# Turned SwiGLU values finished behind later weight tiles, and embedding products kept in DRAM

## The chip, the cores and the metric

The kernel runs on one core of a Trainium2 chip. The metric is device time in microseconds (us) of one execution, as a median of several runs. The engines are named as in the profile: PE multiplies matrices (PEld is its loading of stationary operands), DVE and ACT are the vector and the scalar engine, POOL is the general one, and SP issues most of the DMAs.

## The reference

A trunk of two layers is computed for one sequence of 256 tokens with 1024 channels, in float32. Layer 0 has a mixer (a gated convolution and a gated delta rule), a dense SwiGLU and a gated per-layer embedding; layer 1 has a mixer (differential attention and a convolution module), a SwiGLU with eight experts of which each token uses two, and again a gated embedding. The change lies in the experts and in the embedding of layer 1:

```python
def swiglu(hn, w_gate_up, w_down):
    g, u = jnp.split(hn @ w_gate_up, 2, axis=-1)
    return (jax.nn.silu(g) * u) @ w_down

# each expert e of 8: w_gate_up[e] is 1024 x 7168, w_down[e] is 3584 x 1024
y = lax.map(expert_block, (rows, blk_e))          # swiglu of the rows of expert e
out = jnp.zeros((T, D)).at[tok_s].add(y[dest] * g_s[:, None])

def per_layer_embed(h, p_i, g_norm, w_proj, w_gate):
    gate = jax.nn.sigmoid(rmsnorm(h, g_norm) @ w_gate)
    return (p_i @ w_proj) * gate
```

## The kernel before

All weights come from DRAM once, in tiles of 1 MB (`raw`, 11 buffers), on SP's DMA queue. Products are made with float32 numbers split in two parts of a shorter format: `wsplit` (L135 ff.) lets ACT copy 1024 columns into the high part (`wh`, names h_...) and DVE subtract it to get the low part (`wl`, names l_...). Each of the two has four buffers, which come free when PE has used them. A tile of weights thus costs one ACT copy, one DVE subtraction and several PE products.

The experts run one after the other, each in four chunks of hidden channels (`CHUNKS`: 1024, 1024, 1024, 512). Experts 0 to 3 hold up to 128 tokens ("many"): three products for each tile (high with high, high with low, low with high). Experts 4 to 7 (`FEW`) hold up to 64 tokens, and both parts of the tokens stand beside each other as 128 columns, so that two products do.

A step (e, c) of the loop (L1340 ff.) has two halves. `gate_up` multiplies the tokens with the gate and up weights of chunk c, channel tile by channel tile (k = 0 to 7), into PSUM tiles mg and mu. Then `down` multiplies the values of the chunk before with its down weights (names d..., tiles y). In between stands `mid`, called at k = `MID` = 1, which works on the values of the chunk before (`h_T`):

- many: PE transposes the values (tile mt, L1220), ACT and DVE split them (mhh, mhl, L197 and L198);
- few: ACT has copied gate and up out of PSUM (msg, msu, L1188); PE turns both with small matmuls against `both`, which also adds the two parts (tile mt), four pieces for each of gate and up; ACT takes Silu (mgu, L1211), DVE multiplies (mgu, L1212), and both split the product (mh, L197 and L198). A block is 512 channels, so a chunk of 1024 has two blocks, mt520 and mt521 for expert 5, chunk 2.

The scheduler sets the order on each engine from the order in which the program issues the work and from priorities; an engine runs its instructions strictly in that order, so one that waits holds all behind it. `after(...)` pins an instruction behind a named one. The turn of the chunk (e, c) thus lies in the step after it, among the down tiles of the chunk before (e, c): mt520 is made in step (5, 3) while the tiles d5_1 are being multiplied, and h_T's instructions stand on ACT and DVE in the midst of the copies and splits of these tiles.

The embedding products p @ w_proj of layer 1 (pj1, four tiles of 128 x 512) are made near the start of the experts, are copied to SBUF by ACT (L387) and stay there in four of the twelve `s2` buffers until the end. The last down block (r_dl, L1264) and the gate weights of the embedding (r_pg, r_pg1h) follow behind the experts.

Of the kernel before, what the change touches and what calls it, by code (L numbers as in the profile page):

```python
# [24 lines left out]
NE = 8  # L25
# [58 lines left out]
def trunk_kernel(  # L84
# [6 lines left out]
    pe, act, dve, pool, sync = nc.tensor, nc.scalar, nc.vector, nc.gpsimd, nc.sync  # L91
# [5 lines left out]
    dr = ctx.enter_context(tc.tile_pool(name="dr", bufs=1, space=bass.MemoryType.DRAM))  # L97
# [75 lines left out]
    def mm(o, a, b, start, stop, shared=False):  # L173
        last["mm"] = pe.matmul(o, a, b, start=start, stop=stop, skip_group_check=shared)  # L174
# [768 lines left out]
    def layer1_moe(pT):  # L943
# [110 lines left out]
        def few(e):  # L1054
            return e >= FEW
# [106 lines left out]
        def products(e, triples, start, stop):  # L1162


            if not few(e):
                return mm3s(triples, start, stop)
            for part in range(2):
                for o, a, b in triples:
                    mm(o, a, b[part], start and part == 0, stop and part == 1)

        def gate_up(e, c, mid):
            ns = CHUNKS[c][1] // 512
            banks = [[pa(f"m{nm}{e}{c}{i}") for i in range(ns)] for nm in "gu"]
            for k, j, wt in gate_up_weights(e, c):
                if (k, j) == (MID, 0):
                    mid()
                products(e, [(banks[j][i], tokens[e][k], sub2(wt, slice(None), slice(i * 512, i * 512 + 512))) for i in range(ns)],
                         k == 0, k == KT - 1)

            def activate():  # L1180

                res = []
                with after("wcopy", "wsplit"):
                    for i in range(ns):
                        if few(e):
                            res.append([s2(f"ms{nm}{e}{c}{i}", [P, 512]) for nm in "gu"])
                            for j in range(2):
                                act.copy(res[i][j], banks[j][i])  # L1188
                            continue
                        sg = s2(f"msg{e}{c}{i}", [P, 512])  # L1190
                        act.activation(sg, banks[0][i], AF.Silu)
                        dve.tensor_tensor(sg, banks[1][i], sg, MUL)
                        res.append(sg)
                return res

            return activate

        def h_T(e, c, sgs):

            res = []  # L1200

            for i, sg in enumerate(sgs):
                if few(e):

                    q = pt(f"mt{e}{c}{i}", (P, 2, 4, P // 2))
                    for j in range(2):
                        for g in range(2):
                            for k in range(2):
                                mm(q[:, j, 2 * g + k, :], sg[j][:, 256 * g + k : 256 * g + 256 : 2], both, True, True)
                    t = s2(f"mgu{e}{c}{i}", [P, 4, P // 2])  # L1210
                    act.activation(t, q[:, 0], AF.Silu)  # L1211
                    dve.tensor_tensor(t, q[:, 1], t, MUL)  # L1212
                    hT = s2(f"mh{e}{c}{i}", [P, 4, 2, P // 2], F32R)
                    split((hT[:, :, 0], hT[:, :, 1]), t)
                    res += [hT[:, k].rearrange("q i s -> q (i s)") for k in range(4)]
                    continue
                q = pt(f"mt{e}{c}{i}", (P, 4, P))
                for g in range(2):
                    for k in range(2):
                        pe.transpose(q[:, 2 * g + k, :], sg[:, 256 * g + k : 256 * g + 256 : 2], ident)  # L1220
                hT = (s2(f"mhh{e}{c}{i}", [P, 4, P], F32R), s2(f"mhl{e}{c}{i}", [P, 4, P], F32R))
                split(hT, q)
                res += [sub2(hT, slice(None), k) for k in range(4)]
            return res

        def down(e, c, hT, yb, between):

            c0, n = CHUNKS[c]
            res = None
            for g in range(n // 256):  # L1230
# [3 lines left out]
                for i in range(2):  # L1234
                    products(e, [(yb[half], hT[2 * g + i], sub2(wt[i], slice(None), HALF[half])) for half in range(2)],
                             c == g == i == 0, c == len(CHUNKS) - 1 and g == n // 256 - 1 and i == 1)
                if g == n // 512 - 1 and between:
                    res = between()
            return res
# [100 lines left out]
        prev = None  # L1340
        for e in range(NE):
            for c in range(len(CHUNKS)):
                if e % 2 == 1 and c == 2 and e <= FEW - 1:
                    spread_slots = gather(e // 2 + 1)
                if (e, c) == (FEW, 1):
                    spread_slots()

                def mid():
                    if prev:
                        hT[prev] = h_T(*prev, sg)  # L1350
                    if (e, c) == (0, LATE):
                        for bn in todo:
                            product(*bn, pt)
                            copy(*bn)

                activate = gate_up(e, c, mid)
                if prev:
                    sg = back(*prev, activate)
                else:
                    sg = activate()  # L1360
                    with after("wsplit"):
                        gates()
                prev = e, c
# [129 lines left out]
```

## Time and profile before

| | |
|---|---|
| median of 3 runs | 1497.5 us (1496.99 to 1498.06) |
| profiled execution | 1497.28 us, of which span 1495.5 us |
| PE busy | 1444.5 us (97%) |
| PEld busy | 1194.7 us (80%) |
| DVE busy | 1268.0 us (85%) |
| ACT busy | 1076.1 us (72%) |
| DMA | 438 MB, mean 293 GB/s |
| granted PE clock | 0.995 |

The span is the profiled part of one execution; the rest, 1.8 us, lies around it. A busy share is a mean over stretches with different limits, so the rows further down are taken by stretch: the experts 0 to 3 lie at about 530 to 1005 us, the experts 4 to 7 at about 1005 to 1450 us. In a timeline, a row "x6" is six instructions of one kind in a row; the time in brackets is how long the engine was idle before, and behind the arrow stands what released it.

### The profile page before, as it was taken

The numbers are of one execution on the slowest core, as the hardware profiler recorded it, in microseconds if no ns is written. First come the engines' busy times: TensorE is split into PE (matmuls) and PEld (weight loads), VectorE is DVE, ScalarE is ACT, GpSimd is POOL, SyncE is SP. The second block draws the span as 40 slices with busy tenths as digits, with TensorE's granted clock in tenths as the row PEclk, the third lists the DMA queues.
The fourth block names the chain that finished last, engine by engine and source line by source line (L and its number), as shares of the span: only waits on it lengthen the run. The fifth ranks groups of instructions, "written<-read, shape, count | busy, mean of one in ns | idle before, by whom it ended". The sixth has DMA issues, their size and how long they took to land.

```text
span 1495.5 us, 22012 instructions
## 1 busy us (share of the span) xinstructions
PE 1444.5 (97%) x7726; PEld 1194.7 (80%) x7726; DVE 1268.0 (85%) x1716; ACT 1076.1 (72%) x1441; POOL 4.9 (0%) x14
## 2 busy tenths in 40 slices
PE   7999999999999999999999999999999999999996
PEld 6999899988888878888888888886766666666665
DVE  6778655556698699999999989989999999999997
ACT  6545544446547678887887877779988988988975
POOL 0000000000000000000000000000000000000000
PEclk9999999999999999999999999999999999999998
DMA  9614656555452469898898998999999999999961
GB/s 350 241 43 131 216 177 196 172 195 185 147 203 106 149 248 354 327 410 333 322 376 336 392 347 341 359 363 389 377 409 414 390 413 410 388 413 408 394 254 44
DMA packets 136610, 438.26 MB, mean 293 GB/s; under 512 B 9067, under 2 KB 34188, under 8 KB 122412
## 3 DMA queue, kind: packets, MB, share of 16 engines
q1 hardware_dynamic: 132960, 433.19, 77.3%
q10 hardware_dynamic: 3148, 2.31, 0.5%
q0 software_dynamic: 384, 1.29, 0.4%
q8 instruction: 62, 1.02, 0.3%
q14 instruction: 56, 0.46, 0.1%
HBM read 434.92 MB, written 1.84 MB: 292 GB/s over the span
## 4 chain that ended last, share of the span: by engine, by line
PE 71%; DVE 18%; issue 4%; ACT 4%; DMA 3%; ACTq 0%; DVEq 0%; POOL 0%; POOLq 0%
PE y L174 14%; PE mg L174 11%; PE mu L174 11%; DVE l L146 11%; PE fu L174 4%; PE fg L174 4%; PE fd L174 4%; PE wo L174 3%; PE pg L174 3%; PE mt L174 2%; DMA r_gu<-in_moe_w_gate_up_dram 2%; DVE l_d L146 2%; PE p L174 1%; PE mt L1220 1%; PE in_og L174 1%
## 5 line engine op out<-in xcount | busy, mean ns | idle before, releaser
L146 DVE TENSOR_TENSOR l<-r_gu,h 128x1024 fp32r<-128x1024 f32 x448 | 526.3, 1218 | 18.1 <-ACT h L145 6.3
L145 ACT CAST h<-r_gu 128x1024 fp32r<-128x1024 f32 x448 | 456.6, 1052 | 60.2 <-PE mu L174 22.4
L146 DVE TENSOR_TENSOR l_d<-r_d,h_d 128x1024 fp32r<-128x1024 f32 x220 | 258.6, 1219 | 16.7 <-ACT h_d L145 10.4
L145 ACT CAST h_d<-r_d 128x1024 fp32r<-128x1024 f32 x220 | 226.8, 1054 | 24.7 <-PE mu L174 10.3
L146 DVE TENSOR_TENSOR l_gu<-r_gu,h_gu 128x1024 fp32r<-128x1024 f32 x44 | 53.8, 1224 | 47.7 <-ACT h_gu L145 47.7
L145 ACT CAST h_gu<-r_gu 128x1024 fp32r<-128x1024 f32 x44 | 46.0, 1048 | 64.2 <-PE fu L174 49.0
L174 PE MATMUL y<-l_d,mh 128*128 128x512 f32 x216 | 75.3, 430 | 3.7 <-DVE l_d L146 3.7
L174 PE MATMUL y<-l_d,mhh 128*128 128x512 f32 x224 | 69.8, 393 | 0.1
L174 PE MATMUL y<-h_d,mh 128*128 128x512 f32 x216 | 69.2, 402 | 0.3
L174 PE MATMUL y<-h_d,mhh 128*128 128x512 f32 x224 | 69.4, 391 | 0.0
L174 PE MATMUL y<-h_d,mhl 128*128 128x512 f32 x224 | 69.1, 390 | 0.0
L174 PEld LDWEIGHTS y<-l_d,mh 128*128 128x128 f32 x216 | 34.4, 188 | 27.4 <-DVE l_d L146 25.1
L146 DVE TENSOR_TENSOR l_fd<-r_fd,h_fd 128x1024 fp32r<-128x1024 f32 x22 | 26.9, 1224 | 27.3 <-ACT h_fd L145 26.3
L174 PE MATMUL fg<-x_ffn0h,h_gu 128*128 128x256 f32 x176 | 49.9, 283 | 0.0
L174 PE MATMUL fu<-x_ffn0h,h_gu 128*128 128x256 f32 x176 | 49.9, 283 | 0.0
L174 PE MATMUL fg<-x_ffn0h,l_gu 128*128 128x256 f32 x176 | 49.9, 283 | 0.0
L174 PE MATMUL fu<-x_ffn0l,h_gu 128*128 128x256 f32 x176 | 49.8, 283 | 0.0
L174 PE MATMUL fu<-x_ffn0h,l_gu 128*128 128x256 f32 x176 | 49.8, 283 | 0.0
L174 PE MATMUL fg<-x_ffn0l,h_gu 128*128 128x256 f32 x176 | 49.8, 283 | 0.0
L174 PEld LDWEIGHTS y<-h_d,mhl 128*128 128x128 f32 x224 | 42.1, 188 | 8.9
L174 PEld LDWEIGHTS y<-l_d,mhh 128*128 128x128 f32 x224 | 41.5, 188 | 9.5 <-DVE l_d L146 1.4
L174 PEld LDWEIGHTS y<-h_d,mhh 128*128 128x128 f32 x224 | 41.8, 188 | 8.9 <-ACT h_d L145 0.4
(719 smaller groups left out, 3673.6 us busy)
## 6 DMA issues: line engine op xcount, KB each, us to landing
r_gu<-in_moe_w_gate_up_dram SPq DMA_DIRECT2D x192, 1024.0 KB, 7.7
r_d<-in_moe_w_down_dram SPq DMA_DIRECT2D x110, 1024.0 KB, 7.7
r_gu<-in_moe_w_gate_up_dram SPq DMA_DIRECT2D x64, 512.0 KB, 6.4
r_gu<-in_ffn_w_gate_up_dram SPq DMA_DIRECT2D x44, 512.0 KB, 4.4
r_fd<-in_ffn_w_down_dram SPq DMA_DIRECT2D x11, 1024.0 KB, 4.9
r_wo<-in_ev_w_out_dram SPq DMA_DIRECT2D x4, 1024.0 KB, 12.8
r_pg<-in_ple_w_gate_dram SPq DMA_DIRECT2D x4, 1024.0 KB, 7.0
r_wo<-in_od_w_out_dram SPq DMA_DIRECT2D x4, 1024.0 KB, 5.0
```

Of the source, the lines that this page charges most:

```text
L145: last["wcopy"] = act.copy(wh, raw[:, i : i + step])
L146: last["wsplit"] = dve.tensor_tensor(wl, raw[:, i : i + step], wh.bitcast(F32), SUB)
L174: last["mm"] = pe.matmul(o, a, b, start=start, stop=stop, skip_group_check=shared)
L1220: pe.transpose(q[:, 2 * g + k, :], sg[:, 256 * g + k : 256 * g + 256 : 2], ident)
```

## The change

`mid` is taken apart into four steps, which a step of the loop calls at four channel tiles of gate and up (`MIDS = (1, 3, 2, 5)`): at k = 1 PE turns the values of a few-token chunk, at k = 3 ACT and DVE make Silu and product, at k = 2 PE transposes the blocks of many-token chunks, and at k = 5 ACT and DVE split. Silu, product and splits are pinned behind the weight copies and splits that were issued last (`after("wcopy", "wsplit")`); the two blocks of a chunk share one tile mgu. A list of blocks (`downs`) takes the place of the loop over chunks; with the numbers given (`RAMP = 0`, `QUAD`, `SLOTS`, `PAIR`) the blocks and the token gathering come in the same order as before. At the end the last chunk is turned outside of the loop. The products pj1 are written to DRAM by ACT's queue at (0, 1), and read again by SP's queue ahead of the last block.

```diff
-        def gate_up(e, c, mid):
+        def gate_up(e, c, at):
...
-                if (k, j) == (MID, 0):
-                    mid()
+                if j == 0 and k in at:
+                    at[k]()
...
-                    t = s2(f"mgu{e}{c}{i}", [P, 4, P // 2])
-                    act.activation(t, q[:, 0], AF.Silu)
-                    dve.tensor_tensor(t, q[:, 1], t, MUL)
-                    hT = s2(f"mh{e}{c}{i}", [P, 4, 2, P // 2], F32R)
-                    split((hT[:, :, 0], hT[:, :, 1]), t)
...
+        def turned(e, c, banks):
+            t = s2(f"mgu{e}{c}", [P, len(banks), 4, P // 2])
+            for i, q in enumerate(banks):
+                act.activation(t[:, i], q[:, 0], AF.Silu)
+                dve.tensor_tensor(t[:, i], q[:, 1], t[:, i], MUL)
+            hidden[e, c] = t
...
+        def h_T(e, c, i, q):
+            if few(e):
+                hT = s2(f"mh{e}{c}{i}", [P, 4, 2, P // 2], F32R)
+                split((hT[:, :, 0], hT[:, :, 1]), hidden[e, c][:, i])
+                return [hT[:, k].rearrange("q i s -> q (i s)") for k in range(4)]
+            hT = (s2(f"mhh{e}{c}{i}", [P, 4, P], F32R), s2(f"mhl{e}{c}{i}", [P, 4, P], F32R))
+            split(hT, q)
+            return [sub2(hT, slice(None), k) for k in range(4)]
...
+            def turn_fresh():
+                if fresh and few(fresh[0]):
+                    banks["fresh"] = turn(*fresh)
+                if now == (0, LATE):
+                    for bn in todo:
+                        product(*bn, pt)
+                        copy(*bn)
+                    for b, i in BLOCKS:
+                        act.dma_start(stored[:, b, i], pj1[b][i])
+            def fresh_turned():
+                if "fresh" in banks:
+                    with after("wcopy", "wsplit"):
+                        turned(*fresh, banks["fresh"])
+            def blocks_across():
+                for d in blocks:
+                    banks[d] = across(*d)
+            def blocks_split():
+                with after("wcopy", "wsplit"):
+                    for d in blocks:
+                        hT[d] = h_T(*d, banks[d])
...
+                activate = gate_up(*now, dict(zip(MIDS, (turn_fresh, fresh_turned, blocks_across, blocks_split))))
...
+        if fresh:
+            turned(*fresh, turn(*fresh))
         last_norm = halves_norm_T("ple1")
-        back(*prev)
+        for b, i in BLOCKS:
+            pj1[b][i] = s2(f"pj1{b}{i}", [P, 512])
+            sync.dma_start(pj1[b][i], stored[:, b, i])
+        hT[downs[0]] = h_T(*downs[0], across(*downs[0]))
+        back(*downs[0])
...
-MID = 1
+MIDS = (1, 3, 2, 5)
+RAMP = 0
+QUAD, SLOTS, PAIR = 14, 17, 6
```

What this does to the order on an engine is shown at three places. On DVE in step (5, 3), the turn of chunk (5, 2), before (l_d5_1_2 and l_d5_1_3 are the splits of the down tiles, l_5_3 those of the gate and up tiles; mgu is the product with Silu, mh the split of it):

```order
L146 TENSOR_TENSOR l_d5_1_2_1_11578<-r_d5_1_2_11571,h_d5_1_2_1_11577 128x1024
L1212 TENSOR_TENSOR mgu520_11633<-mt520_11624,mgu520_11633 128x256
L146 TENSOR_TENSOR l_d5_1_3_0_11592<-r_d5_1_3_11589,h_d5_1_3_0_11591 128x1024
L146 TENSOR_TENSOR l_d5_1_3_1_11596<-r_d5_1_3_11589,h_d5_1_3_1_11595 128x1024
L146 TENSOR_TENSOR l_5_3_0_0_11613<-r_gu5_3_0_11609,h_5_3_0_0_11612 128x1024
L146 TENSOR_TENSOR l_5_3_0_1_11617<-r_gu5_3_0_11609,h_5_3_0_1_11616 128x1024
L198 TENSOR_TENSOR mh520_11636<-mgu520_11633,mh520_11636 128x4x64
L1212 TENSOR_TENSOR mgu521_11648<-mt521_11639,mgu521_11648 128x256
L146 TENSOR_TENSOR l_5_3_2_0_11662<-r_gu5_3_2_11658,h_5_3_2_0_11661 128x1024
L146 TENSOR_TENSOR l_5_3_2_1_11666<-r_gu5_3_2_11658,h_5_3_2_1_11665 128x1024
L198 TENSOR_TENSOR mh521_11651<-mgu521_11648,mh521_11651 128x4x64
```

After:

```order
L146 TENSOR_TENSOR l_d5_1_3_0_11592<-r_d5_1_3_11589,h_d5_1_3_0_11591 128x1024
L146 TENSOR_TENSOR l_d5_1_3_1_11596<-r_d5_1_3_11589,h_d5_1_3_1_11595 128x1024
L146 TENSOR_TENSOR l_5_3_0_0_11613<-r_gu5_3_0_11609,h_5_3_0_0_11612 128x1024
L146 TENSOR_TENSOR l_5_3_0_1_11617<-r_gu5_3_0_11609,h_5_3_0_1_11616 128x1024
L146 TENSOR_TENSOR l_5_3_2_0_11650<-r_gu5_3_2_11646,h_5_3_2_0_11649 128x1024
L146 TENSOR_TENSOR l_5_3_2_1_11654<-r_gu5_3_2_11646,h_5_3_2_1_11653 128x1024
L1216 TENSOR_TENSOR mgu52_11661<-mt520_11624,mgu52_11661 128x256
L1216 TENSOR_TENSOR mgu52_11661<-mt521_11633,mgu52_11661 128x256
L146 TENSOR_TENSOR l_5_3_4_0_11674<-r_gu5_3_4_11670,h_5_3_4_0_11673 128x1024
L146 TENSOR_TENSOR l_5_3_4_1_11678<-r_gu5_3_4_11670,h_5_3_4_1_11677 128x1024
L198 TENSOR_TENSOR mh520_11685<-mgu52_11661,mh520_11685 128x4x64
L198 TENSOR_TENSOR mh521_11688<-mgu52_11661,mh521_11688 128x4x64
```

Both products and both small splits have moved, from the midst of the last down tiles, behind the fourth and the sixth gate and up tile. On ACT the Silus and small copies move in the same way.

On DVE at the turn of chunk (5, 3), in step (6, 0), before:

```order
L146 TENSOR_TENSOR l_d5_2_2_1_11762<-r_d5_2_2_11755,h_d5_2_2_1_11761 128x1024
L1212 TENSOR_TENSOR mgu530_11842<-mt530_11833,mgu530_11842 128x256
L146 TENSOR_TENSOR l_d5_2_3_0_11776<-r_d5_2_3_11773,h_d5_2_3_0_11775 128x1024
L146 TENSOR_TENSOR l_d5_2_3_1_11780<-r_d5_2_3_11773,h_d5_2_3_1_11779 128x1024
L198 TENSOR_TENSOR mh530_11845<-mgu530_11842,mh530_11845 128x4x64
L146 TENSOR_TENSOR l_6_0_0_0_11808<-r_gu6_0_0_11795,h_6_0_0_0_11807 128x1024
L146 TENSOR_TENSOR l_6_0_0_1_11812<-r_gu6_0_0_11795,h_6_0_0_1_11811 128x1024
```

After, with the rows up to the product:

```order
L146 TENSOR_TENSOR l_d5_2_2_1_11761<-r_d5_2_2_11754,h_d5_2_2_1_11760 128x1024
L146 TENSOR_TENSOR l_d5_2_3_0_11775<-r_d5_2_3_11772,h_d5_2_3_0_11774 128x1024
L146 TENSOR_TENSOR l_d5_2_3_1_11779<-r_d5_2_3_11772,h_d5_2_3_1_11778 128x1024
L146 TENSOR_TENSOR l_6_0_0_0_11807<-r_gu6_0_0_11794,h_6_0_0_0_11806 128x1024
L146 TENSOR_TENSOR l_6_0_0_1_11811<-r_gu6_0_0_11794,h_6_0_0_1_11810 128x1024
L146 TENSOR_TENSOR l_6_0_1_0_11825<-r_gu6_0_1_11822,h_6_0_1_0_11824 128x1024
L146 TENSOR_TENSOR l_6_0_1_1_11829<-r_gu6_0_1_11822,h_6_0_1_1_11828 128x1024
L146 TENSOR_TENSOR l_6_0_2_0_11852<-r_gu6_0_2_11849,h_6_0_2_0_11851 128x1024
L146 TENSOR_TENSOR l_6_0_2_1_11856<-r_gu6_0_2_11849,h_6_0_2_1_11855 128x1024
L146 TENSOR_TENSOR l_6_0_3_0_11870<-r_gu6_0_3_11867,h_6_0_3_0_11869 128x1024
L146 TENSOR_TENSOR l_6_0_3_1_11874<-r_gu6_0_3_11867,h_6_0_3_1_11873 128x1024
L1216 TENSOR_TENSOR mgu53_11877<-mt530_11832,mgu53_11877 128x256
```

The product has moved behind eight gate and up tiles of expert 6, and the small split (not in the rows) four tiles further.

On PE at the start of the experts, before (mg and mu are the first gate and up products, oq a transpose):

```order
L174 MATMUL mg000_5574<-h_0_0_1_0_5590,xe0l_5496 128x512
L174 MATMUL mg000_5574<-l_0_0_1_0_5591,xe0h_5495 128x512
L174 MATMUL mg001_5575<-h_0_0_0_0_5400,xe0h_5495 128x512
L174 MATMUL mg001_5575<-h_0_0_0_0_5400,xe0l_5496 128x512
L174 MATMUL mg001_5575<-l_0_0_0_0_5401,xe0h_5495 128x512
L174 MATMUL mg001_5575<-h_0_0_1_0_5590,xe0h_5495 128x512
L174 MATMUL mu000_5576<-h_0_0_0_1_5404,xe0h_5495 128x512
```

After:

```order
L174 MATMUL mg000_5575<-h_0_0_1_0_5591,xe0l_5496 128x512
L174 MATMUL mg000_5575<-l_0_0_1_0_5592,xe0h_5495 128x512
L174 MATMUL pj1_11_5807<-pwh101_5317,pTh1_5152 128x512
L174 MATMUL pj1_11_5807<-pwl101_5318,pTh1_5152 128x512
L174 MATMUL pj1_11_5807<-pwh101_5317,pTl1_5153 128x512
L174 MATMUL pj1_11_5807<-pwh111_5325,pTh1_5152 128x512
L174 MATMUL mg001_5576<-h_0_0_0_0_5400,xe0h_5495 128x512
L174 MATMUL mg001_5576<-h_0_0_0_0_5400,xe0l_5496 128x512
```

Four of the six embedding matmuls of pj1_11 now stand ahead of the products mg001; before, all six stood further on.

## Rows read from the trace of the kernel before

**Rows 1.** Stretches: us; busy of PE, PEld, DVE, ACT, POOL; clock, DMA share, GB/s.

```profile
600.00:1005.00 405.00, 404.85 (x1854) 335.75 (x1853) 376.68 (x371) 320.34 (x349) 0.00 (x0) 1.00 0.93 354
1010.00:1440.00 430.00, 411.08 (x1812) 293.40 (x1811) 412.70 (x411) 378.32 (x457) 0.00 (x0) 1.00 1.01 401
1395.00:1400.00 5.00, 5.00 (x31) 4.42 (x31) 4.07 (x6) 5.00 (x9) 0.00 (x0) 1.00 1.03 430
```

**Rows 2.** Waits, 1005 to 1450: engine, releaser: total us, times, longest.

```profile
ACT mgu L1211 <- PE mt L174: 36.0, 19, 3.4
...
DVE mgu L1212 <- ACT mgu L1211: 8.7, 12, 1.0
...
ACT h L145 <- DMA r_gu<-in_moe_w_gate_up_dram: 0.9, 2, 0.6
```

**Rows 3.** Timeline of DVE in step (5, 3): start, us, operation, [idle before].

```profile
1199.56 6.89 DVE L146 TENSOR_TENSOR l_d<-r_d,h_d 128x1024 fp32r<-128x1024 f32 x6
1207.03 0.42 DVE L1212 TENSOR_TENSOR mgu<-mt,mgu 128x256 f32<-128x256 f32 x1 [0.58 <-ACT mgu L1211]
1207.97 2.36 DVE L146 TENSOR_TENSOR l_d<-r_d,h_d 128x1024 fp32r<-128x1024 f32 x2 [0.51 <-ACT h_d L145]
1210.25 2.37 DVE L146 TENSOR_TENSOR l<-r_gu,h 128x1024 fp32r<-128x1024 f32 x2
...
1215.81 2.35 DVE L146 TENSOR_TENSOR l<-r_gu,h 128x1024 fp32r<-128x1024 f32 x2
```

**Rows 4.** Timeline of PE there: the turn of chunk (5, 2), down products.

```profile
1204.14 0.57 PE L174 MATMUL mt<-both,msg 128*128 128x64 f32 x4
...
1208.73 0.71 PE L174 MATMUL y<-l_d,mh 128*128 128x512 f32 x2
1209.28 0.62 PE L174 MATMUL y<-h_d,mh 128*128 128x512 f32 x2
1209.74 0.63 PE L174 MATMUL y<-l_d,mh 128*128 128x512 f32 x2
```

**Rows 5.** Timeline of ACT there: the first Silu.

```profile
1206.62 0.38 ACT L1211 ACTIVATE mgu<-mt 128x256 f32<-128x256 f32 x1 [2.00 <-PE mt L174]
```

**Rows 6.** Timeline of DVE where chunk (6, 3) is turned.

```profile
1329.45 6.89 DVE L146 TENSOR_TENSOR l_d<-r_d,h_d 128x1024 fp32r<-128x1024 f32 x6
1337.38 0.43 DVE L1212 TENSOR_TENSOR mgu<-mt,mgu 128x256 f32<-128x256 f32 x1 [1.04 <-ACT mgu L1211]
1338.32 2.36 DVE L146 TENSOR_TENSOR l_d<-r_d,h_d 128x1024 fp32r<-128x1024 f32 x2 [0.52 <-ACT h_d L145]
1340.60 0.42 DVE L198 TENSOR_TENSOR mh<-mgu,mh 128x256 fp32r<-128x256 f32 x1
1340.94 5.76 DVE L146 TENSOR_TENSOR l<-r_gu,h 128x1024 fp32r<-128x1024 f32 x5
```

**Rows 7.** Timeline of PE there: the product behind the turn.

```profile
1336.74 0.71 PE L174 MATMUL y<-l_d,mh 128*128 128x512 f32 x2
```

**Rows 8.** Timeline of DVE around the change from expert 3 to 4.

```profile
1005.07 2.35 DVE L146 TENSOR_TENSOR l_d<-r_d,h_d 128x1024 fp32r<-128x1024 f32 x2
1009.84 0.69 DVE L198 TENSOR_TENSOR mhl<-mt,mhh 128x512 fp32r<-128x512 f32 x1 [2.42 <-ACT mhh L197]
...
1013.06 5.76 DVE L146 TENSOR_TENSOR l<-r_gu,h 128x1024 fp32r<-128x1024 f32 x5
```

**Rows 9.** Timeline of PE there: the last down tile of expert 3.

```profile
1013.09 0.63 PE L174 MATMUL y<-h_d,mhl 128*128 128x512 f32 x2
```

**Rows 10.** Timeline of PE at the start of the experts.

```profile
531.11 0.50 PE L174 MATMUL mg<-h,xe0h 128*128 128x512 f32 x1 [0.75 <-ACT pj L387]
```

**Rows 11.** Timeline of SP: DMA issues for the last down block.

```profile
1422.45 3.56 SPq L1264 DMA_DIRECT2D r_dl<-in_moe_w_down_dram  x4
```

**Rows 12.** Timeline of ACT: the first copies of that block.

```profile
1448.56 3.89 ACT L145 CAST h_dl<-r_dl 128x1024 fp32r<-128x1024 f32 x4
```

**Rows 13.** DMA issues on the page: KB each, median us to landing.

```profile
r_d<-in_moe_w_down_dram SPq DMA_DIRECT2D x110, 1024.0 KB, 7.7
```

More of the change, by code (lines that the diff above doesn't have):

```diff
@@ L1196, in gate_up, with turn @@
             return activate
-        def h_T(e, c, sgs):
+        def turn(e, c):
             res = []
[L1202 to L1209, printed above, removed]
-                    t = s2(f"mgu{e}{c}{i}", [P, 4, P // 2])
-                    act.activation(t, q[:, 0], AF.Silu)
-                    dve.tensor_tensor(t, q[:, 1], t, MUL)
-                    hT = s2(f"mh{e}{c}{i}", [P, 4, 2, P // 2], F32R)
-                    split((hT[:, :, 0], hT[:, :, 1]), t)
[L1215 to L1223, printed above, removed]
-            return res
@@ L1226, in down @@
-        def down(e, c, hT, yb, between):
+            for i, sg in enumerate(hidden[e, c]):
+                q = pt(f"mt{e}{c}{i}", (P, 2, 4, P // 2))
+                for j in range(2):
+                    for g in range(2):
+                        for k in range(2):
+                            mm(q[:, j, 2 * g + k, :], sg[j][:, 256 * g + k : 256 * g + 256 : 2], both, True, True)
+                res.append(q)
+            return res
+        def turned(e, c, banks):
[4 more added lines that the diff above has]
+            hidden[e, c] = t
@@ new lines, in across @@
+        def across(e, c, i):
+            if few(e):
+                return None
+            q = pt(f"mt{e}{c}{i}", (P, 4, P))
+            for g in range(2):
+                for k in range(2):
+                    pe.transpose(q[:, 2 * g + k, :], hidden[e, c][i][:, 256 * g + k : 256 * g + 256 : 2], ident)
+            return q
+        def h_T(e, c, i, q):
+            if few(e):
+                hT = s2(f"mh{e}{c}{i}", [P, 4, 2, P // 2], F32R)
[4 more added lines that the diff above has]
+            return [sub2(hT, slice(None), k) for k in range(4)]
@@ L1228, in down @@
+        def down(e, c, i, hT, yb, between):
             c0, n = CHUNKS[c]
-            res = None
-            for g in range(n // 256):
+            for g in range(2 * i, 2 * i + 2):
                 nm = f"d{e}_{c}_{g}"
@@ L1233, in down @@
                 wt = wload(view, (2, D), nm, spare(nm))
[L1234 to L1239, printed above, removed]
+                for k in range(2):
+                    products(e, [(yb[half], hT[2 * (g % 2) + k], sub2(wt[k], slice(None), HALF[half])) for half in range(2)],
+                             c == g == k == 0, c == len(CHUNKS) - 1 and g == n // 256 - 1 and k == 1)
+                if g == 2 * i and between:
+                    between()
         def combine(e, yb, half):
@@ L1249, in combine, with back @@
                 dve.scalar_tensor_tensor(h[:, b, s], q, Gr[:, b, e : e + 1], h[:, b, s], MUL, ADD)
-        yb, hT = {}, {}
+        yb, hT, hidden = {}, {}, {}
         both = sm("both", (P, P // 2))
         dve.tensor_tensor(both, ident[:, : P // 2], ident[:, P // 2 :], ADD)
-        def back(e, c, between=None):
-            if c == 0:
+        def back(e, c, i, between=None):
+            if c == i == 0:
                 yb[e] = [py(f"y{e}{half}") for half in range(2)]
+            part = hT.pop((e, c, i))
             if (e, c) == (NE - 1, len(CHUNKS) - 1):
-                part = hT.pop((e, c))
                 rows = expert(moe_w_down, e)[CHUNKS[c][0] :].rearrange("(g q k) c -> g q k c", k=2, q=P)
@@ L1270, in back @@
                 return
-            res = down(e, c, hT.pop((e, c)), yb[e], between)
+            down(e, c, i, part, yb[e], between)
             if c == len(CHUNKS) - 1:
@@ L1274, in back @@
                     combine(e, yb[e], half)
-            return res
         def more_slots(e, pos):
@@ L1338, in overflow @@
             return over > P, more
[L1340 to L1363, printed above, removed]
@@ L1364, in layer1_moe, with between @@
-        mid()
-        last_norm = halves_norm_T("ple1")
-        back(*prev)
+        gates_up = [(e, c) for e in ORDER for c in range(len(CHUNKS))]
+        downs = [(e, c, n) for e in ORDER for c in range(len(CHUNKS)) for n in range(CHUNKS[c][1] // 512)]
+        stored = dr.tile([P, NB, 2, 512], F32, name="pj1d")
+        fresh = None
+        while gates_up or len(downs) > 1:
+            now = gates_up.pop(0) if gates_up else None
+            step = NE * len(CHUNKS) - len(gates_up) - 1 if now else None
+            n = next((i for i, d in enumerate(downs) if d[:2] not in hidden), len(downs))
+            n = min(1 if now and step < RAMP else 2, n, sum(d[0] == downs[0][0] for d in downs))
+            blocks, downs = downs[:n], downs[n:]
+            if step == QUAD:
+                spread_slots = gather(2)
+            if step == SLOTS:
+                spread_slots()
+            if step == PAIR:
+                gather(1)
+            banks = {}
+            def turn_fresh():
[18 more added lines that the diff above has]
+                        hT[d] = h_T(*d, banks[d])
+            if now:
+                activate = gate_up(*now, dict(zip(MIDS, (turn_fresh, fresh_turned, blocks_across, blocks_split))))
+                def between(now=now, activate=activate):
+                    hidden[now] = activate()
+            else:
+                for f in (turn_fresh, fresh_turned, blocks_across, blocks_split):
+                    f()
+                between = None
+            for i, d in enumerate(blocks):
+                back(*d, between if len(blocks) == 1 else None)
+                if i == 0 and len(blocks) == 2 and between:
+                    between()
+            if not blocks:
+                between()
+            if step == 0:
+                with after("wsplit"):
+                    gates()
+            fresh = now
@@ L1451 @@
 CONV_DVE = (31, 31, 5, 9)
-MID = 1
+MIDS = (1, 3, 2, 5)
+RAMP = 0
+ORDER = (0, 1, 2, 3, 4, 5, 6, 7)
 FEW = 4
+QUAD, SLOTS, PAIR = 14, 17, 6
 X_DVE = (3, 7)
```

## Prediction

> **What bounds the kernel now.** I first cut the run into stretches and read the busy time of each engine in each [rows 1]. In the experts with 128 tokens (600 to 1005 us) the matrix engine PE is busy 404.85 of 405 us: there, no wait of another engine is worth anything. In the experts with 64 tokens (1010 to 1440 us) no engine is full: DVE 412.70, PE 411.08, ACT 378.32 of 430. So what counts there is who waits for whom. The waits [rows 2] show one chain: ACT's Silu (tile mgu, L1211) waits 36.0 us for PE's turn (tile mt), DVE's product waits behind that Silu 12 times for 8.7 us, and each time a weight split l_d waits after it, because ACT could not copy the next h_d while it stood at the Silu. A copy of weights waits for DMA only 0.9 us, so loads do not bound, although the DMA engines are always occupied.
>
> The timelines show one such place in full. In step (5, 3), DVE does six splits from 1199.56, then has 0.58 us of idle time, the product at 1207.03, and 0.51 of idle time [rows 3]; ACT had waited 2.00 us [rows 5]. There are eight of these pairs (the turns of chunks c = 1 and c = 2 of experts 4 to 7). The turn of a c = 3 chunk costs more: 1.04 + 0.52 [rows 6], four times. Turns of c = 0 show no idle time on DVE. Between experts 3 and 4 stands one more of 2.42 us [rows 8].
>
> **The change part by part.**
>
> *The unit.* A split of 1024 columns comes every 1.14 us (two in 1338.32 to 1340.60), a small product or split every 0.34 us (1340.60 to 1340.94) [rows 6]. With these I compare the time a stretch took with its work alone.
>
> *Turns of c = 3.* From 1329.45 to 1340.94 DVE did eight splits, a product and a small split: 8 x 1.14 + 2 x 0.34 = 9.80 of 11.49 us, so 1.69 lost [rows 6]. After the change the small work stands behind eight gate and up tiles of the next expert, and the splits run on. Is there something else that holds them? They need one of four buffers (wl, wh), which PE gives back when it has used the tile. Without the stop, the ninth split would come at 1329.45 + 8 x 1.14 = 1338.57; the fifth tile's product with l_d, which frees its buffer, started at 1336.74 and ended by 1337.45 [rows 7]. So nothing holds them: 1.69 is gained. The last of the four, (7, 3), keeps its old order (there is no next chunk). **3 x 1.69 = 5.1 us.**
>
> *Turns of c = 1 and 2.* From 1199.56 to 1215.81 DVE did 12 splits and 4 small pieces: 12 x 1.14 + 4 x 0.34 = 15.04 of 16.25 us, so 1.21 lost [rows 3]. But this turn has 32 small matmuls, not 16, and PE is at it from 1204.14 to 1208.73, with some products in between [rows 4]. Without the stop DVE ends its eighth split at 1199.56 + 9.12 = 1208.68; the ninth needs the buffer of the fifth tile, whose product y<-l_d starts only at 1208.73 and ends at 1209.44. The tenth needs ACT's copy into the buffer of the sixth tile, free at 1209.90 (y<-h_d from 1209.28); at 1.05 us for a copy alone ([rows 12]: four in 3.89, so 0.95 in a row) it is there by 1210.95. So the ninth ends at 1210.58, the tenth at 1212.09, the twelfth at 1214.37, and with 4 x 0.34 the same work is done at 1215.73 instead of 1215.81. The idle time changes its releaser and stays: 0.1 each, **8 x 0.1 = 0.8 us**. The bounds are 0 and the whole 1.21, eight times 9.7; I take the low end since the products' times are read from this very stretch, where PE did not wait for DVE.
>
> What a rule says to this: repeated idle time on DVE is charged by the trace to ACT's Silu [rows 2]. The Trainium skill, "Perfetto Trace Analysis", § Optimization Strategy, says that the same gap coming again on the engine that should be full can mean too few buffers for the next tile. For c = 1 and 2 this is what the times of PE's products give; for c = 3 they speak against it. By the rule for all places no turn would gain, which is the second rival.
>
> *Between experts 3 and 4.* DVE lost 2.42 before mhl and 0.25 behind it. Afterwards mhl stands behind twelve tiles of expert 4. Here too the buffers set the end: the eighth split from 1005.07 on began at 1013.06 + 3 x 1.14 = 1016.48 [rows 8] without the two stops before it; afterwards it needs the buffer of the last h_d, free when the product that starts at 1013.09 ends, 1013.72 [rows 9], and a copy of 0.95, so 1014.7. 1.8 less the 0.69 of mhl, which comes later, is 1.1; that last product itself waited a little for l_d, which is gone, so I take **1.4 us** (bounds 0 and 2.42 + 0.25 - 0.69 = 2.0).
>
> *Start of the experts.* PE was idle 0.75 us for ACT's copy of pj [rows 10]. In the new order four embedding matmuls of the same length that came later stand there. PE has no other slack until 1005, so **0.75, say 0.8 us** (bounds 0 and 1.1).
>
> *The 128-token experts.* Splits of turned blocks move behind later tiles. PE has 0.15 us of idle time in 405 [rows 1], the count of instructions stays, and the first use is three tiles further on: 0.
>
> *Embedding products in DRAM.* Four writes of 256 KB on ACT's DMA queue near 540 us, and four reads on SP's, which stand among the four loads r_dl and ahead of the last weights r_pg. No row shows a write by ACT; by SP's issues (four in 3.56 us [rows 11]) they take at most 3.6 us of ACT, in a stretch in which ACT is idle a fifth of the time [rows 1] and runs ahead of PE by up to four tiles: 0, bounds 0 and 2. The reads wait for the turn of (7, 2), since they take the buffers of its inputs. That turn is over about two experts of 107.5 us (430 for four) after 1208.73, near 1424. So the loads behind them start some 5 us late, near 1428, and land 8 to 9 later [rows 13]; the first copies of r_dl run at 1448.56 [rows 12]. 11 us are left over: 0.
>
> **Sum:** 5.1 + 0.8 + 1.4 + 0.8 = 8.1. Against the profiled execution's 1497.3 (span 1495.5 and 1.8 around it; median of the runs 1497.5, 0.2 more) that is 1489.2; on the median **1489.4**. By the bounds of all terms: low with 9.7 + 5.1 + 2.0 + 1.1, high with 5.1 less 2.
>
> **The rivals.**
>
> *All the idle time goes.* If the order of PE's products in the turns gives buffers back earlier than I read, 8 x 1.2 + 5.1 + 2.0 + 0.8 = 17.5 are gained: 1480.0. For it: the releaser named in the rows. Against it: the product at 1208.73. DMA would stand it: 401 GB/s become 418 over the stretch, and the fastest of 86 windows of 5 us moved 430 [rows 1].
>
> *The idle time comes back everywhere at the buffers.* Then the turns of c = 3 give nothing either, and only the start and the place between the experts are left: 1497.5 - 2.2 = 1495.3. For it: PE falls behind in every turn. Against it: the release by 1337.45 [rows 7], 1.1 us before it is needed.
>
> *Slower: Silu and split now stand in front of ACT's copies just where DVE takes them from its hand.* At the tenth split of step (5, 3) ACT has no lead at all (above); from there it gains 1.14 - 0.95 = 0.19 a tile, so some 0.8 us at the fourteenth, where two Silus stand together. If that lead were gone, each Silu and small split of 27 blocks would stop DVE for its 0.38 us [rows 5]: 27 x 2 x 0.38 = 20.5, and 1497.5 - 8.1 + 20.5 = 1510. It decides against the change once two fifths of them do so. Against it: ACT has 52 us of idle time in the 430 [rows 1], much of it the waits for the turn that go away.
>
> **How the numbers follow.** My forecast 0.58 (alone 1486 to 1493), all idle time gone 0.18, back at the buffers 0.16, slower 0.08. What a measurement of this kernel can tell from no change is about 0.2%, 3 us. Faster by more: 0.58 + 0.18 = 0.76; within: 0.16; slower by more: 0.08. The range reaches from the first rival to a little above the second, 1480 to 1496, and leaves out the slower case.
>
> **What would show it.** In the trace afterwards: the product behind the Silu no longer in DVE's waits, except at (7, 3); DVE without idle time at the c = 3 turns of experts 4 to 6; at c = 1 and 2 about 0.8 and 0.4 us in front of the first two gate and up splits, released by PE's y products and ACT's copy; PE without the stop for pj. Wrong would be: idle time on DVE behind ACT's Silu or copies at the third to fifth gate and up tile (slower rival), idle time at the c = 3 turns (second rival), or none at c = 1 and 2 (first).

## The result, and the profile after

The changed kernel takes **1488.5 us** (median of 4 runs, 1488.33 to 1488.63) against 1497.5 us before: a ratio of 0.9943, with a 95% interval of 0.9929 to 0.9957. The forecast was 1489.4 us. The profiled execution has a span of 1486.7 us, 8.8 us less than before.

To see where the time went, I took one mark for each expert from the timelines of DVE, the first addition of the expert's result into h (the first row h<-cb of each expert), and set the two traces beside each other. For expert 4 these are the rows, before and after:

```profile
1150.35 1.40 DVE L1249 SCALAR_TENSOR_TENSOR h<-cb,Gr,h 128x512 f32<-128x512 f32 x2
1145.69 1.40 DVE L1260 SCALAR_TENSOR_TENSOR h<-cb,Gr,h 128x512 f32<-128x512 f32 x2
```

| first h<-cb of expert | before, us | after, us | ahead by | gained since the mark above |
|---|---|---|---|---|
| 0 | 675.61 | 674.84 | 0.77 | 0.77 |
| 1 | 800.04 | 799.18 | 0.86 | 0.09 |
| 2 | 920.13 | 918.87 | 1.26 | 0.40 |
| 3 | 1040.73 | 1037.62 | 3.11 | 1.85 |
| 4 | 1150.35 | 1145.69 | 4.66 | 1.55 |
| 5 | 1259.49 | 1253.00 | 6.49 | 1.83 |
| 6 | 1368.60 | 1360.31 | 8.29 | 1.80 |
| 7 | 1456.20 | 1447.82 | 8.38 | 0.09 |
| end of span | 1495.5 | 1486.7 | 8.8 | 0.4 |

Each of the intervals that end at experts 4, 5 and 6 holds one turn of c = 3 and two of c = 1 and 2; the interval of expert 7 holds two turns of c = 1 and 2 and the last turn, which keeps its order. It gains 0.09 us.

The waits between 1000 and 1445 us answer [rows 2] (engine and tile, releaser: total, times, longest). ACT's wait at the Silu for PE's turn has shrunk from 36.0 us to 14.5, and DVE's wait behind that Silu from 12 times to 2. In their place ACT's weight copies wait for PE's y products, and DVE's splits wait for these copies:

```profile
ACT h L145 <- PE y L174: 24.5, 26, 1.3
...
ACT mgu L1215 <- PE mt L174: 14.5, 8, 3.3
...
DVE l L146 <- ACT h L145: 9.5, 19, 0.8
...
DVE mgu L1216 <- ACT mgu L1215: 1.5, 2, 1.0
```

The timeline of DVE in step (5, 3), where chunk (5, 2) is turned, answers [rows 3]. Eight splits l_d run without a stop now; then the first split of a gate and up tile waits 0.80 us and the second 0.26; both products and both small splits come later, without a wait:

```profile
1194.85 9.17 DVE L146 TENSOR_TENSOR l_d<-r_d,h_d 128x1024 fp32r<-128x1024 f32 x8
1204.81 1.23 DVE L146 TENSOR_TENSOR l<-r_gu,h 128x1024 fp32r<-128x1024 f32 x1 [0.80 <-ACT h L145]
1206.30 3.50 DVE L146 TENSOR_TENSOR l<-r_gu,h 128x1024 fp32r<-128x1024 f32 x3 [0.26 <-ACT h L145]
1209.71 0.75 DVE L1216 TENSOR_TENSOR mgu<-mt,mgu 128x256 f32<-128x256 f32 x2
```

ACT in the same place stands in front of the copies of those two tiles and waits for PE to give back the buffers:

```profile
1203.12 1.05 ACT L145 CAST h<-r_gu 128x1024 fp32r<-128x1024 f32 x1 [1.31 <-PE y L174]
1205.21 2.95 ACT L145 CAST h<-r_gu 128x1024 fp32r<-128x1024 f32 x3 [1.05 <-PE y L174]
```

PE has the same order as in [rows 4]: the last of the turn, then the products at 1204.00 and 1204.55. The former ends at 1204.71, and the first split starts at 1204.81; the profile names ACT's copy as its releaser, but that was done at 1204.17, so it is PE's product that gave the buffer back. The latter ends at 1205.17, ACT's second copy starts at 1205.21, and the second split behind it:

```profile
1203.09 1.11 PE L174 MATMUL mt<-both,msu 128*128 128x64 f32 x8
1204.00 0.71 PE L174 MATMUL y<-l_d,mh 128*128 128x512 f32 x2
1204.55 0.62 PE L174 MATMUL y<-h_d,mh 128*128 128x512 f32 x2
```

At the turn of c = 3 (here of expert 6, answering [rows 6]) DVE has no stop any more: eight l_d and eight gate and up splits run in a row, and the product comes behind them:

```profile
1322.90 9.16 DVE L146 TENSOR_TENSOR l_d<-r_d,h_d 128x1024 fp32r<-128x1024 f32 x8
1331.98 9.17 DVE L146 TENSOR_TENSOR l<-r_gu,h 128x1024 fp32r<-128x1024 f32 x8
1341.07 0.42 DVE L1216 TENSOR_TENSOR mgu<-mt,mgu 128x256 f32<-128x256 f32 x1
```

Between experts 3 and 4, the stop of 2.42 us [rows 8] has become three shorter ones, again in front of the splits that need a copy:

```profile
1003.09 4.92 DVE L146 TENSOR_TENSOR l_d<-r_d,h_d 128x1024 fp32r<-128x1024 f32 x4
1008.41 1.23 DVE L146 TENSOR_TENSOR l<-r_gu,h 128x1024 fp32r<-128x1024 f32 x1 [0.40 <-ACT h L145]
1010.02 1.23 DVE L146 TENSOR_TENSOR l<-r_gu,h 128x1024 fp32r<-128x1024 f32 x1 [0.38 <-ACT h L145]
1011.40 11.67 DVE L146 TENSOR_TENSOR l<-r_gu,h 128x1024 fp32r<-128x1024 f32 x10 [0.16 <-ACT h L145]
```

At the start of the experts, PE goes from the last of the four embedding matmuls to mg001 without the stop of [rows 10]. A second stop of that stretch is left, with 0.52 us; before it was 0.98 us long (second fence, from the trace of before):

```profile
531.36 0.40 PE L174 MATMUL pj<-pwh,pTh 128*128 128x512 f32 x1
531.59 0.48 PE L174 MATMUL mg<-h,xe0h 128*128 128x512 f32 x1
...
553.44 0.50 PE L174 MATMUL mg<-h,xe0h 128*128 128x512 f32 x1 [0.52 <-ACT msg L1192]
```

```profile
552.84 0.50 PE L174 MATMUL mg<-h,xe0h 128*128 128x512 f32 x1 [0.98 <-ACT msg L1191]
```

By stretch (columns as in [rows 1]), PE is still full in the 128-token experts, and DVE is busier in the 64-token ones, 414 of 428 us:

```profile
600.00:1003.00 403.00, 403.00 (x1848) 335.10 (x1847) 376.74 (x372) 319.84 (x350) 0.00 (x0) 1.00 0.95 356
1003.00:1431.00 428.00, 407.42 (x1835) 300.54 (x1834) 414.24 (x413) 374.97 (x458) 0.00 (x0) 1.00 1.02 406
```

### The profile page after: what moved, and what is told of

It is laid out like the page before. It is cut to its first block, busy times and chain, and to the rows that moved or that the text cites. A ratio compares the mean times of both kernels' runs of the same rounds, so it can differ in the third digit from the quotient of the medians.

```text
span 1486.7 us, 22047 instructions
## 1 busy us (share of the span) xinstructions
PE 1436.4 (97%) x7726; PEld 1198.6 (81%) x7726; DVE 1267.1 (85%) x1716; ACT 1070.9 (72%) x1441; POOL 4.9 (0%) x14
## 4 chain that ended last, share of the span: by engine, by line
PE 77%; DVE 14%; ACT 3%; issue 3%; DMA 2%; ACTq 0%; DVEq 0%; POOL 0%; POOLq 0%
PE y L174 16%; PE mu L174 13%; PE mg L174 13%; DVE l L146 8%; PE fu L174 4%; PE fg L174 4%; PE fd L174 4%; PE mt L174 3%; PE wo L174 3%; PE pg L174 3%; PE p L174 1%; DMA r_gu<-in_moe_w_gate_up_dram 1%; PE mt L1226 1%; PE in_og L174 1%; PE xg L174 1%
## 5 line engine op out<-in xcount | busy, mean ns | idle before, releaser
L174 PE MATMUL mu<-l,xe2l 128*128 128x512 f32 x112 | 40.9, 435 | 11.2 <-DVE l L146 10.5
```

## The experiments

The theory: two things hold DVE at a turn, one behind the other. The first is the order, in which ACT stands at a Silu until PE has turned; the change takes it away. The second is the four split buffers, which PE does not give back while it turns; it takes over at once where the turn has 32 small matmuls (c = 1 and 2), and does not where it has 16 (c = 3). The rivals: each moved Silu gives an equal part; or the stops left over come from ACT's order or from the loads.

**Only c = 3 late.** `early_turn` does Silu, product and split at k = 1, block by block, as before.

```diff
...
-                if fresh and few(fresh[0]):
+                if fresh and few(fresh[0]) and fresh[1] != 3:
+                    early_turn(*fresh)
+                elif fresh and few(fresh[0]):
                     banks["fresh"] = turn(*fresh)
...
```

> Only the last chunk (c = 3) of the 64-token experts keeps its Silu, product and split behind the later tiles; for c = 0, 1 and 2 they stand where the kernel before had them. Theory of the buffers (PE's turn of 32 matmuls keeps the four split buffers at c = 1 and 2, so moving Silu there gains 0.1 us each): 1488.5 + 8 x 0.1 = 1489.3 us. Rival, that every one of the 11 stops gave an equal part of the 5.2 us gained in the 64-token experts (0.47 each): eight of them come back, 1492.3 us.

Measured: 1488.67 us (1487.58 to 1488.96), a ratio of 0.9938 (0.9925 to 0.9952). The marks of experts 4 to 7 are 107.9, 107.4, 107.4 and 87.6 us apart, as with the whole change. The old stops are there again at c = 1 and 2, and cost what the new ones cost (timeline of DVE, turn of (5, 1)):

```profile
1172.45 0.42 DVE L1228 TENSOR_TENSOR mgu<-mt,mgu 128x256 f32<-128x256 f32 x1 [0.58 <-ACT mgu L1227]
1173.38 2.36 DVE L146 TENSOR_TENSOR l_d<-r_d,h_d 128x1024 fp32r<-128x1024 f32 x2 [0.51 <-ACT h_d L145]
```

So 24 of the 27 moved blocks of the 64-token experts gain nothing that the time shows; the rival of equal parts (1492.3) falls.

**All but c = 3 late.** The same edit with `fresh[1] == 3`.

> The reverse: only c = 3 keeps the old place of Silu, product and split; c = 0, 1 and 2 have the new one. Theory of the buffers: the three turns of c = 3 lose 1.69 us each again, 1488.5 + 5.1 = 1493.6 us. Rival of equal parts: 3 x 0.47 come back, 1489.9 us.

Measured: 1492.88 us (1492.31 to 1493.55), ratio 0.997 (0.9958 to 0.9982). The marks of experts 4, 5 and 6 are 109.8, 109.0 and 109.0 us apart, 1.7 more each than with the whole change, 5.2 in all. The old stops at c = 3 (turn of (4, 3)):

```profile
1115.37 0.43 DVE L1228 TENSOR_TENSOR mgu<-mt,mgu 128x256 f32<-128x256 f32 x1 [1.02 <-ACT mgu L1227]
1116.31 2.36 DVE L146 TENSOR_TENSOR l_d<-r_d,h_d 128x1024 fp32r<-128x1024 f32 x2 [0.52 <-ACT h_d L145]
```

**PE's turn of c = 3 twice as long.** The values stay the same, since each small matmul is only made again.

```diff
+                            for again in range(2 if c == 3 and e < NE - 1 else 1):
                                 mm(q[:, j, 2 * g + k, :], sg[j][:, 256 * g + k : 256 * g + 256 : 2], both, True, True)
```

> The changed kernel with PE's turn of c = 3 of experts 4 to 6 made twice, one after the other into the same place (32 small matmuls in place of 16; the values stay the same). Theory of the buffers: the idle time of 0.80 + 0.26 us that c = 1 and 2 have now comes at c = 3 too, 3 x 1.06: 1488.5 + 3.2 = 1491.7 us. Rival, that the number of small matmuls does not matter: 1488.5 us.

Measured: 1490.88 us (1490.33 to 1492.46), ratio 0.9962 (0.9948 to 0.9976); that is 2.4 us more than the change alone by the medians and 2.8 by the ratios (0.9962 against 0.9943). The marks of experts 4 to 6 are 109.1, 108.4 and 108.3 apart, 1.0 more each, 3.1 in all. The stop appears at c = 3, in front of the first gate and up splits (turn of (5, 3)), of about the size it has at c = 1 and 2:

```profile
1217.18 9.16 DVE L146 TENSOR_TENSOR l_d<-r_d,h_d 128x1024 fp32r<-128x1024 f32 x8
1226.27 1.21 DVE L146 TENSOR_TENSOR l<-r_gu,h 128x1024 fp32r<-128x1024 f32 x1
1227.68 1.23 DVE L146 TENSOR_TENSOR l<-r_gu,h 128x1024 fp32r<-128x1024 f32 x1 [0.21 <-ACT h L145]
1229.55 3.50 DVE L146 TENSOR_TENSOR l<-r_gu,h 128x1024 fp32r<-128x1024 f32 x3 [0.64 <-ACT h L145]
```

**A fifth split buffer.**

```diff
-RAW_BUFS = 11
+RAW_BUFS = 10
...
-SPL_BUFS = 4
+SPL_BUFS = 5
```

> Five split buffers instead of four, paid for by ten raw buffers instead of eleven; nothing else. Theory of the buffers: the ninth split then waits for the fourth tile's product and not the fifth's, which PE ends before its turn is over, so the eight pairs of 0.80 + 0.26 us go: 1480.0 us. Rival, that the buffers don't hold it: 1488.5 us. Rival, that ten raw buffers are too few for the loads: slower than 1488.5 us, with ACT waiting for DMA.

Measured: **1479.0 us** (1478.77 to 1479.12), ratio 0.9877 (0.9862 to 0.9892). The marks of experts 4 to 7 are 105.6, 105.1, 105.1 and 85.3 apart, 2.2 to 2.5 less each than with four buffers (two pairs of 0.80 + 0.26 are 2.1). In the timeline of DVE in step (5, 3) no stop is left, while ACT still waits for PE at the same two copies; DVE has one tile more in hand:

```profile
1190.63 9.16 DVE L146 TENSOR_TENSOR l_d<-r_d,h_d 128x1024 fp32r<-128x1024 f32 x8
1199.72 4.74 DVE L146 TENSOR_TENSOR l<-r_gu,h 128x1024 fp32r<-128x1024 f32 x4
1204.38 0.75 DVE L1216 TENSOR_TENSOR mgu<-mt,mgu 128x256 f32<-128x256 f32 x2
```

```profile
1198.91 1.05 ACT L145 CAST h<-r_gu 128x1024 fp32r<-128x1024 f32 x1 [1.31 <-PE y L174]
1201.01 2.01 ACT L145 CAST h<-r_gu 128x1024 fp32r<-128x1024 f32 x2 [1.05 <-PE y L174]
```

**Its control: ten raw buffers alone.** Only `RAW_BUFS = 10`.

> The changed kernel with ten raw buffers instead of eleven and four split buffers as it has: the control of the run with five split buffers. Theory: loads do not bound, 1488.5 us, within 1, so that all of the 9.5 us there belong to the split buffer. Rival, that less is in flight: slower, with ACT waiting for DMA by more than the 2.1 us it has in the changed kernel from 1000 to 1445.

Measured: 1489.22 us (1488.52 to 1490.25), ratio 0.9943 (0.993 to 0.9957), the ratio of the change itself. So the 9.5 us are the split buffer's.

**The fifth buffer without the change.** The same two numbers in the kernel before.

> The kernel before the change with five split buffers and ten raw buffers. If two things hold DVE at the turns of c = 1 and 2 in turn, the order (ACT standing at its Silu for PE's turn) and then the buffers, the fifth buffer alone gains next to nothing: 1497.1 us, at most 1 less. Rival, that a fifth buffer alone is worth what it was worth on top of the change (9.5 us of 1488.5 to 1479.0): 1487.6 us.

Measured: 1496.64 us (1496.02 to 1497.84), ratio 0.9997 (0.9988 to 1.0007). Nothing is gained: in step (5, 3) DVE stops as in [rows 3], and ACT, which has a buffer more to fill, only stands longer at its Silu, 2.94 us instead of 2.00 [rows 5]:

```profile
1206.04 0.42 DVE L1212 TENSOR_TENSOR mgu<-mt,mgu 128x256 f32<-128x256 f32 x1 [0.58 <-ACT mgu L1211]
1206.97 2.36 DVE L146 TENSOR_TENSOR l_d<-r_d,h_d 128x1024 fp32r<-128x1024 f32 x2 [0.51 <-ACT h_d L145]
```

```profile
1205.62 0.38 ACT L1211 ACTIVATE mgu<-mt 128x256 f32<-128x256 f32 x1 [2.94 <-PE mt L174]
```

Order and buffers lie in series. The buffer alone gives 0. The order alone gives about 0.05 us for a turn of c = 1 or 2: the marks of experts 5 and 6 are 0.09 us nearer to each other with the whole change than with c = 3 alone late, for two such turns each. Both together give 1.15 (an expert takes 105.1 us instead of 109.1, of which 1.7 are the turn of c = 3).

**The turn taken apart.** In the 64-token experts, the first block is turned at k = 1, the second at k = 5, both pinned behind PE's last product; Silu follows at k = 6, the split at k = 7.

```diff
...
-                activate = gate_up(*now, dict(zip(MIDS, (turn_fresh, fresh_turned, blocks_across, blocks_split))))
+                activate = gate_up(*now, {1: turn_fresh, 2: blocks_across, 5: lambda: (second_turn(), blocks_split(False)), 6: fresh_turned, 7: lambda: blocks_split(True)})
...
```

> The turn of a chunk with two blocks is taken apart: 16 small matmuls at k = 1 behind the products issued last, 16 at k = 5, Silu and product at k = 6, split at k = 7, for the 64-token experts alone. Theory of the buffers: with half a turn in one piece, as at c = 3, PE gives the split buffers back in time, the idle times of 0.80 and 0.26 us on DVE go away eight times: 1488.5 - 8.5 = 1480.0 us. Rival, that the idle time at c = 1 and 2 comes from the order of ACT's copies and not from how long PE is at the turn: 1488.5 us, within 1. Second rival, that the loads bound there: idle time on DVE moves to places where ACT waits for DMA, 1486 to 1488.5 us.

Measured: 1483.12 us (1481.99 to 1483.44), ratio 0.9902 (0.9887 to 0.9918): 5.4 us less than the change, not the 8.5 expected. The stops in front of the first gate and up splits are gone, so a turn in two pieces does not hold the split buffers. (The pin also puts both pieces behind other products than before, and this run does not tell the two apart; the run with c = 3 made twice varies the length alone.) But new stops came at the turn of c = 2. Its step has half as many gate and up tiles, so Silu follows soon behind the second half of the turn. ACT waits 1.56 us at the second Silu until PE has turned, and the Silu and the copies behind it stop DVE (timelines of ACT and DVE, step (5, 3)):

```profile
1210.50 0.39 ACT L1217 ACTIVATE mgu<-mt 128x256 f32<-128x256 f32 x1 [1.56 <-PE mt L174]
```

```profile
1201.11 9.19 DVE L146 TENSOR_TENSOR l<-r_gu,h 128x1024 fp32r<-128x1024 f32 x8
1210.22 0.42 DVE L1218 TENSOR_TENSOR mgu<-mt,mgu 128x256 f32<-128x256 f32 x1
1210.92 0.42 DVE L1218 TENSOR_TENSOR mgu<-mt,mgu 128x256 f32<-128x256 f32 x1 [0.28 <-ACT mgu L1217]
1211.26 0.98 DVE L198 TENSOR_TENSOR mh<-mgu,mh 128x256 fp32r<-128x256 f32 x2
1212.77 9.39 DVE L146 TENSOR_TENSOR l_d<-r_d,h_d 128x1024 fp32r<-128x1024 f32 x8 [0.52 <-ACT h_d L145]
```

4 x (0.28 + 0.52) = 3.2 us, which is 8.5 less 5.4 within 0.1. That it meets so closely is in part luck, since smaller differences are not in this sum: a stop of 0.86 us that DVE has ahead of each expert's mark in the changed kernel is 0.53 here for experts 4 to 6, and the eight splits behind the new stops take 9.39 us instead of 9.17. What stops DVE here is the old order on a smaller scale, ACT standing at a Silu for PE's turn, and not the third rival of the prediction, in which Silus stop DVE because ACT has no lead.

**The 128-token blocks early again.** Transposes and splits of experts 0 to 3 are issued at k = 1.

```diff
+                for d in blocks:
+                    if not few(d[0]):
+                        hT[d] = h_T(*d, across(*d))
                 if now == (0, LATE):
...
```

> Blocks of the 128-token experts are transposed and split at k = 1 again, as before; all else as changed. The 1.85 us between experts 3 and 4 and the 1.2 us at the start (the blocks' transposes again stand ahead of the last embedding product) come back: 1488.5 + 3.1 = 1491.6 us. Rival, that the start's 1.2 us come from the writes to DRAM and not from the blocks: 1490.4 us.

Measured: 1491.31 us (1490.92 to 1493.54), ratio 0.9964 (0.9951 to 0.9976), 2.8 us more than the change. Both stops of PE at the start are back at their old lengths, so they hang on the blocks and not on the writes to DRAM, and so is the stop of 2.42 us between experts 3 and 4. From the mark of expert 0 to that of expert 2 it takes 244.6 us, as before (244.5), and not the 244.0 of the change, so 0.5 us of the 128-token experts come from these blocks as well (timelines of PE and DVE):

```profile
533.00 0.50 PE L174 MATMUL mg<-h,xe0h 128*128 128x512 f32 x1 [0.75 <-ACT pj L387]
554.69 0.50 PE L174 MATMUL mg<-h,xe0h 128*128 128x512 f32 x1 [0.98 <-ACT msg L1192]
```

```profile
1011.76 0.69 DVE L198 TENSOR_TENSOR mhl<-mt,mhh 128x512 fp32r<-128x512 f32 x1 [2.42 <-ACT mhh L197]
```

**Embedding products in SBUF.** Without the four writes and four reads.

```diff
-                    for b, i in BLOCKS:
-                        act.dma_start(stored[:, b, i], pj1[b][i])
...
-            pj1[b][i] = s2(f"pj1{b}{i}", [P, 512])
-            sync.dma_start(pj1[b][i], stored[:, b, i])
```

> The changed kernel with the embedding products kept in SBUF as before (no writes to DRAM, no reads; four of the twelve s2 buffers stay taken). Theory: writes and reads are hidden and the buffers are not scarce, so 1488.5 us, within 1. Rival, that the eight s2 buffers left are too few for values that now live longer: slower, with stops on ACT for released buffers; second rival, that the DRAM traffic costs something in the tail: up to 2 us faster.

Measured: 1489.41 us (1488.59 to 1489.73), ratio 0.9944 (0.9931 to 0.9958), the same as the change. The move to DRAM neither gains nor costs here.

**Fifth buffer and a later last turn.** On top of the fifth buffer, the last chunk's Silu and product are pinned behind the last weight splits.

```diff
-        if fresh:
+        with after("wcopy", "wsplit"):
             turned(*fresh, turn(*fresh))
+            hT[downs[0]] = h_T(*downs[0], across(*downs[0]))
...
```

> Five split buffers, ten raw buffers, and the last chunk's Silu and product pinned behind the last weight splits too, its split right behind. DVE's stops at the last turn (1.03 + 0.51 us) go: 1479.0 - 1.5 = 1477.5 us. Rival, that the last products are then late for the end of the experts and it comes back there: 1479.0 us.

Measured: 1479.71 us (1477.71 to 1481.22), ratio 0.9889 (0.9874 to 0.9905), not told apart from the fifth buffer alone. DVE's two stops at the last turn are gone, but from the first h<-cb of expert 7 to the end of the span it takes 40.7 us (1435.03 to 1475.7) instead of 38.8 (1437.97 to 1476.8), so what was gained came back at the end. The fastest version seen is the change with five split buffers.

## Why the prediction was right

- **The start of the experts** was given 0.8 us. PE's stop of 0.75 went whole, and 0.46 of a second stop that I had not costed, 1.2 in all. The first mark shows only 0.77 of it, since this execution came to the experts 0.47 us later (the transpose oq began at 529.76 instead of 529.29). No edit lies ahead of that, and in the traces of the other runs on the changed kernel oq begins anywhere from 528.95 to 531.19, so this is a spread between executions. That 0.77 meets the 0.8 is luck.
- **The 128-token experts** were given 0; between the marks of experts 0 and 2 it is 0.5 us. The run with their blocks early again takes it back, so moving these blocks gave it, although PE's idle time there was only 0.15 us. By which waits stays open.
- **Between experts 3 and 4**: 1.4 expected, 1.85 measured between the marks. The buffers set the end, as worked out; the stops left are 0.40, 0.38 and 0.16.
- **Turns of c = 3 and of c = 1 and 2**: 5.1 + 0.8 = 5.9 expected, 1.55 + 1.83 + 1.80 + 0.09 = 5.3 measured. The part of c = 3 is shown by undoing it alone (5.2 us back). That of c = 1 and 2 was taken too high: about 0.05 a turn instead of 0.1. The stops that I had worked out from PE's products, about 0.8 and 0.4 us, came with 0.80 and 0.26. Expert 4 gained 0.3 less than the others. DVE waits there for the second Silu of the first chunk, which I had counted as free; with c = 0, 1 and 2 early again this stop is gone and the interval gains 1.69 against before, nearly as much as the others (1.74). My signs had named (7, 3) as the only place where DVE would still wait behind a Silu, so this one is a miss:

```profile
1048.55 0.42 DVE L1216 TENSOR_TENSOR mgu<-mt,mgu 128x256 f32<-128x256 f32 x1 [0.47 <-ACT mgu L1215]
```

- **The embedding products in DRAM**: 0 expected and 0 shown. The four reads stood in SP's queue from 1415.62 for 3.59 us. Most of that is waiting for the turn of (7, 2), as I had expected, and the loads behind them came about 4 us later, well ahead of their use (waits of SP's queue, 1412 to 1424):

```profile
SPq L1417 <- PE mt L174: 3.0, 4, 1.0
```

- **The end** gave 0.4 us, which I had not counted; the order of its small pieces differs a little, and what gave it is not shown.

So the mechanism was right, and the sum is a little better than its terms. By the marks, 8.8 us were gained where 8.1 were counted: the 128-token experts, the place between experts 3 and 4 and the end gave 1.4 more in all, and the turns 0.6 less.

The choice that decided was to take the low end, 0.1 of 1.2 us, for eight of the eleven stops. The waits alone, which name ACT's Silu as the releaser [rows 2], would have led to the first rival (1480.0 us). The Trainium skill ("Perfetto Trace Analysis", § Optimization Strategy) names too few buffers for the next tile as a possible cause of a gap that keeps coming back. Here that was so at c = 1 and 2, as the second of two limits, and not at c = 3, where DVE has no stop with the same four buffers. What separated the two was a count, in the trace of before, of when PE ends with the tile whose buffer the ninth split needs: 0.76 us after DVE would want it at c = 1 and 2 (1209.44 against 1208.68), 1.1 us before at c = 3.

## What to carry to other kernels

An idle time has the releaser that came last, and taking that away gains only up to the next one in line; before moving a step, walk each engine's order on without it and see when the buffers it then needs come back. Where two limits lie in series, changing either alone shows nothing (a fifth buffer alone 0.9997, the new order alone about 0.05 us a turn), while both together gave 9.5 us more than the order; so a change that gains little at a place can be worth keeping for the next one. Where an engine returns buffers, look at how long its other work stands in one piece: here a turn of 32 small matmuls stopped DVE for 1.06 us, one of 16 did not, and the 32 in two pieces did not stop it for buffers.

## What the runs showed of the hardware

With five split buffers the loads no longer kept pace, which the waits hardly show. An expert of 64 tokens then takes 105.1 us instead of the 107.3 of the change, and by the shapes its weights are 44.04 MB, so it uses them up at 419 GB/s (an estimate) instead of 410. But from the mark of expert 4 to that of expert 6 the DMA engines moved 410 GB/s with four buffers and 411 with five (the last two numbers are DMA share and GB/s; first the change, then with five buffers):

```profile
1146.00:1361.00 215.00, 204.23 (x914) 149.07 (x915) 209.01 (x210) 188.02 (x230) 0.00 (x0) 1.00 1.02 410
1143.00:1353.00 210.00, 201.58 (x913) 149.29 (x913) 208.15 (x209) 186.35 (x229) 0.00 (x0) 1.00 1.02 411
```

So the rest must have come out of the lead that the loads had (argued from the rates; no run isolates it). They also took longer: from issue to landing, a gate and up tile needed 14.9 us in the median (1100 to 1380) instead of 9.4, and 9.1 with ten raw buffers alone. ACT's copies still waited for loads only 3.6 us in 445. The prediction took 418 GB/s to be safe since single windows of 5 us had moved up to 430; such a peak did not tell what lasts, and whether more experts could run at this pace is not shown.

The issue of a read of 256 KB took SP 0.32 us. That four of them filled 3.59 us of its queue was due to the wait for PE's turn.
